# Decoder step: other paces for the background decode in the projection (7.0 to 6.4) and in the second attention (15.0 to 45)

## The chip, the cores and the metric

The kernel runs on one core of a Trainium2 chip. The metric is the device time of one launch in microseconds. The engines are TensorE (PE in the profile; PEld is its weight load), VectorE (DVE), ScalarE (ACT), GpSimd (POOL) and SyncE (SP); SP, ACT and POOL also issue DMAs.

## The reference, cut to what matters

One layer of a decoder is computed for two groups at once: a prompt of 1024 rows, and 8 sample rows that are decoded against a paged cache of 8192 past positions each.

```python
h = rmsnorm(x) @ w_in                       # q, k, v, forget logits, u, z
att = softmax(q k^T/8 + cq - ck) v          # causal, 8 heads of 64
sgu = u * (tril(w_s) z + b_s)               # gating in chunks of 128
x = x + concat(rmsnorm(att), rmsnorm(sgu)) @ w_o
x = x + cross_attend(rmsnorm(x), 256 memory tokens)
x = x + conv_ffn(rmsnorm(x))                # width 2 * 2816, conv of 3
y = rmsnorm(x)
# sample rows: the same layer, with att over the pages of the cache
k_all = concat(cache_k[page_table], k); v_all = concat(cache_v[page_table], v)
```

All values are float32. The outputs are both groups' y, the new k, v, log forget gates and the convolution's states.

## The kernel before, in words

The prompt is the main work. It goes through stages, each a Python generator: `p1` (the input projection, w_in in column groups of 512, with x split in a high and a low part, so that each product is three matmuls), `attention(0)` for rows 0 to 511 mixed with the memory's keys and the gating, `attention(1)` for rows 512 to 1023, and then for each half of the rows `merge` (the normed attention and gating rows are turned by TensorE and split, L860 and L212/L213), `out_proj` (w_o, L973 to L975), `cross` and `ffn`. The stages bear the names p1, att0, att1, mid0 (merge to cross of the first half), ffn0, mid1 and ffn1. A weight block is loaded by SP into one of four `wr` tiles (L223) and split by ScalarE (L209) and VectorE (L210) into `wh` and `wl`. The probability rows of the second attention use the same `wr` tiles.

The sample group's decode is the background. `decode()` has 148 steps. Step g loads, by an indirect DMA on POOL's queue (L1306), one K tile of 128x2048 into one of the four `kv` tiles. VectorE multiplies it by the query (L1312) and reduces it by heads (L1316); in the two attention stages each of the two operations is cut in halves (KS = 2), elsewhere it is done whole. Eighteen steps behind, the step loads one V tile into the same four `kv` tiles (L1365); every second step TensorE multiplies two V tiles (L1371, 16 matmul records). At the end of 16 steps, one sample row's pages, the softmax follows in small pieces over the next steps. After the decode, `sample_rest` does the remaining layer for the sample rows, with L1653 its last large product.

The order comes from the loop that drives both. Each yield of the main generator gives a number, about the microseconds of TensorE that were issued. The loop adds it to an account, and issues a step of the background when the account has reached the pace of the stage, which it then subtracts. Per yield it issues at most `int(t / pace) + 1` steps.

```python
acc[0] += t
most = int(t / PACE[phase[1] or phase[0]]) + 1
while bgs and not held[0] and most and acc[0] >= PACE[phase[1] or phase[0]]:
    most -= 1
    acc[0] -= PACE[phase[1] or phase[0]]
    if next(bgs[0], None) is None:
```

The yields of p1 sum to 210.0 (16 of 2.6, 8 of 5.2 in the groups Q and Z, 8 of 5.4, 16 of 5.2, 4 of 0.1), those of att0 with its fill to 124.2, those of att1 to 74.6; merge yields 0.5 eight times, and out_proj 2.6 eight times for its first column half. What is left in the account at the end of a stage is carried into the next. With the paces before, p1 issues 30 steps (0 to 29), att0 6 (30 to 35) and att1 5 (36 to 40); 3.8 units are carried on, and step 41 is issued after out_proj's first yields.

What is issued is put in order for each engine by a scheduler that goes by priority (the order of issue) among the instructions that are ready by its own model of time; the order is fixed when the kernel is built. A K step's VectorE instructions are bound behind the newest VectorE instruction that had been issued before it (`behind(ENG.DVE)`), and the value products likewise on TensorE. `close(1)`, which norms the second attention's rows, runs beside the first half's merge.

Of the kernel before, what the change touches and what calls it, by code (L numbers as in the profile page):

```python
# [72 lines left out]
KS = 2  # L73
BKQ = 1
LA = (2, 2)
PACE = {'p1': 7.0, 'att0': 20.0, 'mid0': 8.0, 'ffn0': 8.5, 'att1': 15.0, 'mid1': 6.8, 'ffn1': 2.5, 'rest': 2.9}


def build(nc, tc, ctx, a, phases=None):
# [1684 lines left out]
    for t in prompt():  # L1764
# [6 lines left out]
# [6 lines that stand above are left out]
# [94 lines left out]
```

## Time and the profile before

| what | value |
|---|---|
| median of 3 runs | 1911.37 us |
| lowest, highest | 1909.26, 1916.39 us |
| profiled execution, its own time | 1913.18 us |
| its span, first to last instruction | 1911.4 us |
| mean granted TensorE clock | 0.978 |
| HBM read, written | 493.63 MB, 21.84 MB |

In the rows of the profile a group is line, engine, operation, out<-in with shapes, count, then busy time in us and mean ns of one, then the idle time of the engine just before these instructions and what ended it. In a row by windows stand the stretch, its length, the busy time of PE, PEld, DVE, ACT and POOL with instruction counts, the granted TensorE clock, the share of time in which the 16 DMA engines were busy, and GB/s. In a row of waits stand the total in us, how often, and the longest. In a row in order of time stand start, duration, the instruction, and in brackets the idle time before it and what ended it.

### The profile page before, as it was taken

Reading aid. Unit: us, or ns where it says so; the run is one execution under the profiler, and the core shown is the slowest. Engines: PE = TensorE matmul, PEld = TensorE weight load, DVE = VectorE, ACT = ScalarE, POOL = GpSimd, SP = SyncE. Lnnn points to the kernel's source line nnn. Section 1 sums busy time; section 2 is a strip of 40 time slices with the busy share of each in tenths; the row PEclk is TensorE's granted clock in tenths of the full one; section 3 lists DMA queues with packets and bytes.
Section 4 is the critical chain, followed back from the end, with each engine's and each line's share of the span. In section 5 each row is a group of like instructions: output and inputs, shape, how many; then the busy total and the mean of one; then the engine's idle time right before and its main releaser. Section 6 shows DMA issues by size and latency. Waiting matters only on the chain.

```text
span 1911.4 us, 24216 instructions
## 1 busy us (share of the span) xinstructions
PE 1816.1 (95%) x9255; PEld 1296.3 (68%) x9255; DVE 1404.6 (73%) x1662; ACT 761.7 (40%) x1435; POOL 480.6 (25%) x429
## 2 busy tenths in 40 slices
PE   8999999778898999999999999998999999899998
PEld 5987666555676667777777776775665667667765
DVE  4888678777777887989989998887864548754344
ACT  5332356566633435333333244324353333232232
POOL 1232342222121332213432322354222012101110
PEclk9999999989998999999999999998999999899999
DMA  8777988743395876759878879888859557676872
GB/s 322 286 245 278 323 319 302 265 162 119 128 399 210 324 268 256 297 206 359 313 264 313 301 304 344 340 338 302 307 206 362 191 200 265 215 242 247 320 280 101
DMA packets 156373, 517.07 MB, mean 271 GB/s; under 512 B 20169, under 2 KB 41929, under 8 KB 123489
## 3 DMA queue, kind: packets, MB, share of 16 engines
q0 software_dynamic: 56400, 339.04, 47.7%
q1 hardware_dynamic: 92944, 163.89, 24.7%
q10 hardware_dynamic: 6912, 12.59, 1.7%
q8 instruction: 73, 1.20, 0.2%
q14 instruction: 44, 0.35, 0.1%
HBM read 493.63 MB, written 21.84 MB: 270 GB/s over the span
## 4 chain that ended last, share of the span: by engine, by line
PE 66%; DVE 8%; ACT 3%; DMA 3%; issue 2%; POOL 0%; SPq 0%; DVEq 0%; POOLq 0%; ACTq 0%
PE ba L247 9%; PE ba L246 9%; PE ba L248 9%; PE bb L246 6%; PE bb L247 5%; PE bb L248 5%; PE dv L1371 5%; DMA kv<-cache_k,kidx 2%; DVE kv L1312 1%; DVE s L1316 1%; PE dv L1614 1%; PE ba L973 1%; PE ba L975 1%; PE ba L974 1%; PE bb L772 1%
## 5 line engine op out<-in xcount | busy, mean ns | idle before, releaser
L209 ACT ACTIVATE wh<-wr 128x1024 fp32r<-128x1024 f32 (+2 forms) x220 | 228.8, 1044 | 488.8 <-PE ba L247 147.8
L210 DVE TENSOR_TENSOR wl<-wr,wh 128x1024 fp32r<-128x1024 f32 (+2 forms) x220 | 262.5, 1200 | 166.7 <-PE ba L248 71.3
L1306 POOL DMA_INDIRECT kv<-cache_k,kidx x128 | 179.8, 1405 | 545.6 <-DVE s L1316 249.3
L1312 DVE TENSOR_TENSOR kv<-kv,d 128x2048 f32<-128x2048 f32 (+1 forms) x139 | 292.3, 2113 | 28.2 <-DMA kv<-cache_k,kidx 26.9
L1316 DVE TENSOR_REDUCE s<-kv 128x32 f32<-128x2048 f32 (+1 forms) x139 | 292.0, 2106 | 0.6
L1365 POOL DMA_INDIRECT kv<-cache_v,kidx x128 | 181.3, 1416 | 424.2 <-PE dv L1371 169.6
L246 PE MATMUL ba<-wh,u 128*128 128x512 f32 (+1 forms) x596 | 226.9, 382 | 0.0
L247 PE MATMUL ba<-wl,u 128*128 128x512 f32 (+1 forms) x596 | 226.2, 380 | 0.0
L248 PE MATMUL ba<-wh,u 128*128 128x512 f32 (+1 forms) x596 | 223.4, 380 | 1.0 <-DVE u L210 1.0
L246 PE MATMUL ba<-u,wh 128*128 128x512 f32 (+2 forms) x520 | 203.0, 391 | 1.3 <-DVE u L213 1.2
L247 PE MATMUL ba<-u,wh 128*128 128x512 f32 (+2 forms) x520 | 203.8, 392 | 0.0
L248 PE MATMUL ba<-u,wl 128*128 128x512 f32 (+2 forms) x520 | 202.7, 390 | 0.0
L1371 PE MATMUL dv<-kv,s 128*32 128x512 f32 x1024 | 138.0, 618 | 6.8 <-DMA kv<-cache_v,kidx 6.8
L246 PE MATMUL bb<-u,wh 128*128 128x512 f32 (+2 forms) x344 | 138.2, 402 | 1.8 <-DVE u L213 1.8
L247 PE MATMUL bb<-u,wh 128*128 128x512 f32 (+2 forms) x344 | 136.5, 397 | 2.5 <-DVE u L213 2.5
L248 PE MATMUL bb<-u,wl 128*128 128x512 f32 (+2 forms) x344 | 135.9, 396 | 0.0
L246 PEld LDWEIGHTS ba<-wh,u 128*128 128x128 f32 x596 | 112.7, 189 | 31.4 <-issue 8.0
L248 PEld LDWEIGHTS ba<-wh,u 128*128 128x128 f32 x596 | 112.1, 189 | 29.0 <-issue 6.3
L247 PEld LDWEIGHTS ba<-wl,u 128*128 128x128 f32 x596 | 112.4, 189 | 23.8 <-issue 2.9
L247 PEld LDWEIGHTS ba<-u,wh 128*128 128x128 f32 x520 | 98.7, 190 | 33.3 <-issue 13.0
L246 PEld LDWEIGHTS ba<-u,wh 128*128 128x128 f32 x520 | 98.5, 190 | 31.7 <-issue 7.1
L248 PEld LDWEIGHTS ba<-u,wl 128*128 128x128 f32 x520 | 98.5, 189 | 28.5 <-issue 9.3
(418 smaller groups left out, 3105.5 us busy)
## 6 DMA issues: line engine op xcount, KB each, us to landing
wr<-w_up SPq DMA_DIRECT2D x88, 512.0 KB
kv<-w_up POOLq DMA_DIRECT2D x22, 1024.0 KB
wr<-w_down SPq DMA_DIRECT2D x40, 512.0 KB
kv<-w_down POOLq DMA_DIRECT2D x11, 1024.0 KB
wr<-w_in SPq DMA_DIRECT2D x16, 512.0 KB
wr<-w_o SPq DMA_DIRECT2D x16, 512.0 KB
wr<-w_cq SPq DMA_DIRECT2D x16, 512.0 KB
wr<-w_co SPq DMA_DIRECT2D x16, 512.0 KB
```

What stands on the lines that cost most here:

```text
L209: nc.scalar.activation(h, src, AF.Copy)
L210: nc.vector.tensor_tensor(l, src, h.bitcast(F32), op=ALU.subtract)
L246: mmul(out, sh, mh, start=(i == 0), stop=False)
L247: mmul(out, sh, ml, start=False, stop=False)
L248: mmul(out, sl, mh, start=False, stop=(i == n - 1))
L772: mmul(po[64 * j : 64 * j + 64, q0:256], vn[:, kt, 64 * j : 64 * j + 64], pt[j][kt // 4][:, kt % 4, q0:256], start=(kt == 0), stop=(kt == ...
L973: mmul(pss[i], mh[k][:, tb], wh, start=(k == korder[0]), stop=False)
L1306: nc.gpsimd.indirect_dma_start(kv, None, a["cache_k"], off(kidx[:, b, ch : ch + 1]))
L1312: nc.vector.tensor_tensor(kvv[:, i : i + m, :], kvv[:, i : i + m, :], qb.unsqueeze(1).broadcast_to((P, m, 512)), op=ALU.mult)
L1316: nc.vector.tensor_reduce(s[:, ch * 4 + i : ch * 4 + i + m, :].rearrange("p k h -> p (k h)"), kvv[:, i : i + m, :].rearrange("p k (h d) -> ...
L1365: nc.gpsimd.indirect_dma_start(kv, None, a["cache_v"], off(kidx[:, b, ch : ch + 1]))
L1371: mmul(dv[32 * j : 32 * j + 32, :], s[:, ch * 4 : ch * 4 + 4, :].rearrange("p k h -> p (k h)"), kvv[:, j, :], start=(ch == 0), stop=(ch == ...
```

## The change

Two entries of the pace table get other values. No instruction's work is altered apart from one thing: a K step that is issued in a stage other than the two attentions is done in whole instead of half operations.

```diff
-PACE = {'p1': 7.0, 'att0': 20.0, 'mid0': 8.0, 'ffn0': 8.5, 'att1': 15.0, 'mid1': 6.8, 'ffn1': 2.5, 'rest': 2.9}
+PACE = {'p1': 6.4, 'att0': 20.0, 'mid0': 8.0, 'ffn0': 8.5, 'att1': 45, 'mid1': 6.8, 'ffn1': 2.5, 'rest': 2.9}
```

By the loop's arithmetic p1 then issues 32 steps (204.8 of 210.0 units), att0 6 and att1 one; 39.0 units are carried into mid0, whose pace is 8.0, and each of the merge's first five yields issues a step. All later steps move with them.

## The prediction, made before the changed kernel was run

> **What bounds the kernel now.** First the page's totals and slices, for the engine that sets the end and the places where it does not run.
>
> ```profile
> PE 1816.1 (95%) x9255; PEld 1296.3 (68%) x9255; DVE 1404.6 (73%) x1662; ACT 761.7 (40%) x1435; POOL 480.6 (25%) x429
> PE   8999999778898999999999999998999999899998
> PE 66%; DVE 8%; ACT 3%; DMA 3%; issue 2%; POOL 0%; SPq 0%; DVEq 0%; POOLq 0%; ACTq 0%
> ```
>
> TensorE is busy 95% of the span and is two thirds of the chain that ended last. The change adds and removes no matrix work, so its effect is in the other 5%, and in time at a lowered clock. The dip in the slices lies at about 250 to 525 us, the two attentions. The view by windows separates the stages around the change: projection, second attention, merge and first output projection, and what follows; then three short stretches of the attention and one of the last stage.
>
> ```profile
> core 0: us, PE busy (x) PEld busy (x) DVE busy (x) ACT busy (x) POOL busy (x), PEclk, DMA share, GB/s
> 13.00:250.00 237.00, 236.92 (x1271) 184.90 (x1271) 170.24 (x152) 89.39 (x137) 67.72 (x49) 1.00 0.81 292
> 405.00:520.00 115.00, 94.00 (x625) 66.06 (x626) 82.28 (x169) 72.97 (x195) 22.52 (x31) 0.91 0.40 134
> 520.00:550.00 30.00, 29.05 (x156) 20.73 (x157) 25.20 (x29) 13.06 (x21) 8.75 (x6) 1.00 1.03 401
> 550.00:575.00 25.00, 25.00 (x117) 18.68 (x116) 17.00 (x15) 7.40 (x17) 5.26 (x4) 1.00 0.95 375
> 420.00:430.00 10.00, 7.30 (x38) 5.72 (x39) 6.29 (x16) 5.79 (x16) 0.96 (x1) 0.68 0.76 243
> 440.00:450.00 10.00, 7.21 (x49) 4.80 (x48) 8.26 (x15) 6.46 (x15) 2.25 (x3) 0.83 0.31 104
> 490.00:500.00 10.00, 6.04 (x35) 4.49 (x34) 6.66 (x16) 5.06 (x16) 1.03 (x1) 0.83 0.32 108
> 1424.00:1500.00 76.00, 76.00 (x384) 45.65 (x383) 39.64 (x59) 28.12 (x45) 16.29 (x18) 1.00 0.86 318
> ```
>
> Three things are to be seen. The projection keeps TensorE busy 236.92 of 237 us: every matmul put there is paid in full. The second attention idles it 21 of 115 us at a mean clock of 0.91, with DMA at 40%: this stage has something to win. The merge stretch (520 to 550 us) is full on all sides: TensorE 29.05, VectorE 25.20 of 30 us, DMA saturated at 401 GB/s. What leaves the attention late lands there.
>
> The waits of TensorE within 405 to 520 us name what it waits for:
>
> ```profile
> PE ba L728 <- DVE mx L736: 6.8, 1, 6.8
> PE bb L756 <- ACT wr L738: 5.0, 2, 4.0
> PE ba L728 <- ACT wr L738: 4.3, 5, 1.6
> PE ms L772 <- ACT t L763: 2.8, 1, 2.8
> ```
>
> Two waits, 6.8 and 4.0 us, are half of the 21. The time-ordered view of VectorE and TensorE shows whose they are.
>
> ```profile
> 413.75 2.34 DVE L1312 TENSOR_TENSOR kv<-kv,d 128x1024 f32<-128x1024 f32 x2
> 417.32 1.21 DVE L1316 TENSOR_REDUCE s<-kv 128x16 f32<-128x1024 f32 x1
> 419.98 1.20 DVE L1316 TENSOR_REDUCE s<-kv 128x16 f32<-128x1024 f32 x1
> 421.82 0.14 DVE L736 TENSOR_TENSOR mx<-mx 128x1 f32<-128x1 f32 x1
> 422.05 0.71 PE L728 MATMUL ba<-u,u 128*128 128x448 f32 x1 [6.78 <-DVE mx L736]
> 439.24 2.35 DVE L1312 TENSOR_TENSOR kv<-kv,d 128x1024 f32<-128x1024 f32 x2
> 460.76 2.35 DVE L1312 TENSOR_TENSOR kv<-kv,d 128x1024 f32<-128x1024 f32 x2
> 487.17 2.35 DVE L1312 TENSOR_TENSOR kv<-kv,d 128x1024 f32<-128x1024 f32 x2
> 490.83 2.33 DVE L1316 TENSOR_REDUCE s<-kv 128x16 f32<-128x1024 f32 x2
> 494.10 0.65 PE L756 MATMUL bb<-cp,wr 128*128 128x128 f32 x4 [3.96 <-ACT wr L738]
> 515.60 2.35 DVE L1312 TENSOR_TENSOR kv<-kv,d 128x1024 f32<-128x1024 f32 x2
> ```
>
> The five starts of L1312 (413.75, 439.24, 460.76, 487.17, 515.60) are the five decode steps of this attention, numbers 36 to 40. The steps at 413.75 and 487.17 sit between a score product and its row maximum, and TensorE waits behind them; the other three are beside other work.
>
> **The change part by part.** *Which steps move.* By the loop's arithmetic (the yields given above) the projection issues steps 0 to 31 instead of 0 to 29, the first attention 32 to 37 instead of 30 to 35, the second attention one step (38) instead of five. At its end 39.0 units are owed, and at pace 8.0 with one step a yield the first five yields of the merge issue steps 39 to 43 in a row. Before, 39 and 40 lie in the attention, and 41 comes after the merge. So the merge stretch gains three steps beyond its own. After it the decode stays about two steps ahead, and reaches the last feed-forward stage at step 131 instead of 129. Step 38 is issued at 370.2 units, near the 376.6 of before (the step at 460.76), so the four that leave are those at 413.75, 439.24, 487.17 and 515.60.
>
> *The attention.* The step at 413.75 spends 2.34 + 1.21 + 1.20 = 4.75 us on VectorE ahead of the L736 that ended the 6.78 us wait; without it some 2.0 us of that wait are left, because L733, L795 and L713 lie there too. The step at 487.17 spends 2.35 + 2.33 = 4.68 us in the same place, more than the wait of 3.96: all of it goes, and ScalarE's exponentials (L738, waits of up to 1.6 us) are next. The steps at 439.24 and 515.60 bring nothing: the first wait behind 439 is ScalarE's L763, and nothing long follows 515. Gain 4.75 + 3.96 = 8.7 us. From below: nothing, if ScalarE is late in both places anyway; from above: these 8.7 and the 2.8.
>
> *The clock.* The windows that hold these waits granted 0.68 and 0.83: 3.2 and 1.7 us of full-speed time lost in 10 us each, 4.9 together. I take half, 2.5, because 440 to 450 us also shows 0.83 though its longest wait is 2.8 us, so a wait cut to 2 us can still cost clock. Ends: 0 and 4.9. The Trainium skill ("TensorE: Matmul & The Clock Gate", What's actually happening) puts the lowered clock behind an idle window of about 3.4 us. By that rule both losses vanish and the sum gains 2.4 us more; the 0.83 behind a wait of 2.8 us speaks against using it as a threshold here.
>
> *The steps' own price elsewhere.* Full-size operations and their neighbours:
>
> ```profile
> L1312 DVE TENSOR_TENSOR kv<-kv,d 128x2048 f32<-128x2048 f32 x117 | 266.5, 2282 | 28.2 <-DMA kv<-cache_k,kidx 26.9 <-PE bb L1106 0.8 <-issue 0.2
> L1316 DVE TENSOR_REDUCE s<-kv 128x32 f32<-128x2048 f32 x117 | 265.7, 2275 | 0.6
> L210 DVE TENSOR_TENSOR wl<-wr,wh 128x1024 fp32r<-128x1024 f32 x208 | 252.0, 1219 | 158.8 <-PE ba L248 70.4 <-PE bb L248 35.0 <-PE ba L247 19.3
> 515.09 1.92 PE L1371 MATMUL dv<-kv,s 128*32 128x512 f32 x16
> 1855.96 1.03 PE L1653 MATMUL ms<-kv,d 128*32 128x512 f32 x4
> ```
>
> A step is 2.28 + 2.28 = 4.56 us of VectorE; every second step a pair of value steps runs on TensorE for 1.92 us; and each step loads one K and, 18 steps behind, one V tile of 1.05 MB on POOL's queue.
>
> *The projection.* Two more steps: 9.1 us of VectorE against 237 - 170 = 67 idle, and about 4 MB, 10 us at 401 GB/s, against a DMA share of 0.81: hidden by TensorE's 237 us. One more value pair on a full TensorE costs 1.9. If the weight splits of L210 were caught behind the steps, the 9.1 would be the upper end; below zero nothing leads, since no wait there can shrink.
>
> *The merge.* Three more steps are 13.7 us of VectorE where 520 to 550 us leaves 4.8 idle: 8.9 over, with the splits of w_o (L210, 1.2 us each) and of the turned rows (L213) in the same queue, and the output projection waiting for both. The two first steps find their tiles loaded, because four KV buffers fill in the attention, whose DMA share is 0.40. The products of the first row blocks cover some of the delay; 25 us later 8 us of VectorE are idle again, but TensorE's lost time is not got back. Ends: 0, all hidden, and 8.9 plus a clock loss of 1.7. I take 7, nearer to the upper end, because 29.05 of 30 us leave no idle time in which to catch up. The value pair of 515.09 moves from the end of the attention to here: TensorE pays it in both places, no net cost.
>
> *The end.* The last stage starts full too (76 of 76 us) and has one value pair less, -1.9, against the +1.9 of the projection. The decode's remainder ends with L1653 at 1857 us, 54 us before the span does, so that an earlier finish brings nothing.
>
> Sum: -8.7 - 2.5 + 1.9 + 7 - 1.9 = -4.2 us. The profiled execution took 1913.2 us (span 1911.4, 1.8 around it); it becomes 1909.0. The median of the runs is 1911.4, 1.8 below the profiled one: 1907.
>
> **The rivals.** *The burst is hidden.* The scheduler may slip steps 39 and 40 into the attention's tail, where VectorE is idle 33 of 115 us, away from row maxima. Then the merge costs nothing and the clock term is whole: -8.7 - 4.9 = -13.6, 1898. For it: order on an engine is by readiness, and the tiles are there. Against: a step is bound behind the newest VectorE instruction issued before it, which for step 39 is already one of the merge.
>
> *The burst stops TensorE.* VectorE runs its queue in order. If the steps that still wait for their tiles stand ahead of the splits of w_o, TensorE has only the row blocks already split. Price: the three steps whole, 13.7, the landing of two tiles, 2.1 MB at 401 GB/s, 5.2, and a clock loss like that of 420 to 430 us, 3.2: 22.1 in place of 7, so +10.9, 1922. It decides from the point at which a step's L1312 with a tile on its way stands ahead of the second w_o split. For it: L1312's 26.9 us of waits for K tiles. Against: these stand over 117 operations, a quarter microsecond each.
>
> *The loads get in each other's way.* Three steps bring 6.3 MB more into a stretch at 401 GB/s; if all of it delays w_o and x, that is 15.7 us in place of the 7: +4.5, 1916. The Trainium skill ("DMA: Bandwidth & Descriptors", Issuing engines are not separate DMA queues) says that transfers share the same 16 engines and interleave whichever engine issued them, which speaks against this change; the saturated 1.03 agrees. Against the full price: four tiles come early, in the attention's idle DMA time.
>
> *Nothing moves.* The steps wait for buffers and data, and so run where they ran: 1911.
>
> **How the numbers follow.** A measurement of this kernel tells about 0.5% from no change, 9.6 us: faster is below 1901.8, slower above 1920.9. Chances: forecast 0.49 (its own range, from the ends of its terms, 1898 to 1914), hidden burst 0.20, stopped TensorE 0.19, loads 0.08, nothing moves 0.04. The range 1895 to 1924 holds the forecast, both rivals' values and leaves out their far ends: a merge dearer still, or a gain beyond 13.6 with other waits of the attention gone. Faster: most of the hidden burst and a corner of the forecast, 0.24. Slower: most of the stopped TensorE and the far end of the loads, 0.22. Same: 0.54.
>
> **What would show it.** In the changed profile the attention should hold one or two L1312 pairs, not five, with the 6.8 and 4.0 us waits at most 2 us and a clock above 0.91; TensorE still 100% busy in the projection; and four or five full-size L1312 close together in the merge, with TensorE waiting a few microseconds on L213 or L210. No such waits means the hidden burst; more than 10 us there, with L1312 waiting for K tiles, the stopped TensorE. The forecast is wrong in its first term if the attention gets no shorter, in its fourth if the merge's loss is not between 0 and 11 us, and in its approach if the difference arises after 610 us.

## The result, and the profile after

The changed kernel takes 1916.54 us (median of 20 runs, 1906.19 to 1925.28), the kernel before 1911.33 us beside it (20 runs, 1906.80 to 1916.39). The ratio is 1.0024, with a 95% interval of 1.0012 to 1.0035: slower by 5 us, within the 0.5% that the prediction counted as no change, and on the other side of zero than its forecast of 1907. The profiled execution took 1917.93 us (span 1916.2, mean clock 0.977) against 1913.18 (1911.4, 0.978).

The page of the kernel after: totals, TensorE's slices and the chain that ended last.

```profile
PE 1817.0 (95%) x9255; PEld 1294.5 (68%) x9255; DVE 1400.5 (73%) x1654; ACT 763.5 (40%) x1435; POOL 496.2 (26%) x429
PE   8999997879989989999999999999999999899998
PE 77%; DMA 8%; DVE 7%; issue 5%; ACT 2%; POOL 0%; SPq 0%; DVEq 0%; POOLq 0%; ACTq 0%
```

The totals say nothing: TensorE is busy for 1816.1 us before and 1817.0 after. TensorE's slices of 47.9 us do: the seventh (287 to 335 us) has gone from 9 to 7, the tenth and eleventh (431 to 527) from 8 to 9, the twelfth (527 to 575) from 9 to 8. Windows of the kernel after, in the order of the prediction's, with the border between projection and first attention added (PE, PEld, DVE, ACT, POOL busy, clock, DMA share, GB/s):

```profile
13.00:250.00 237.00, 235.00 (x1270) 179.36 (x1269) 176.23 (x152) 84.12 (x126) 78.21 (x50) 1.00 0.83 303
290.00:303.00 13.00, 3.57 (x16) 2.12 (x17) 9.54 (x12) 2.27 (x3) 6.50 (x6) 0.53 1.03 403
405.00:520.00 115.00, 103.24 (x697) 73.06 (x696) 77.44 (x187) 86.59 (x237) 19.56 (x29) 0.95 0.32 103
420.00:430.00 10.00, 7.56 (x44) 5.40 (x44) 6.93 (x17) 8.28 (x23) 2.26 (x3) 0.86 0.15 57
520.00:550.00 30.00, 22.92 (x120) 14.71 (x121) 23.64 (x26) 11.62 (x21) 6.72 (x6) 0.83 0.98 371
```

The same 13 us at the border, before:

```profile
290.00:303.00 13.00, 13.00 (x71) 9.69 (x70) 12.68 (x14) 7.97 (x16) 6.02 (x7) 1.00 1.01 399
```

Three things are to be seen. The attention did what was forecast: TensorE busy 103.24 instead of 94.00 of 115 us, clock 0.95 instead of 0.91. The merge lost 6.1 us of TensorE and 0.17 of the clock. And at 290 to 303 us, where the prediction had put no wait at all, TensorE runs 3.57 of 13 us at a clock of 0.53.

To add the stages up, each kernel's main work (all TensorE columns outside the decode) was summed in order of time, and the time compared at which it reaches the amount that before has reached at a given moment. Kernel after: 16.9 us late at 310 us, 1.9 early at 520, 10.2 late at 530, 4.8 late at the end. So projection with its border costs 16.9, the attentions give 18.8 back, the start of the merge takes 12.1, and what follows returns 5.4. At 280 us the main work is 0.5 us late, so the 16.9 arise within 30 us.

The waits of TensorE in the kernel after, first at the border (280 to 310 us), then in the second attention (405 to 520), then in the merge (520 to 550); us in total, times, longest:

```profile
PE ba L677 <- DMA t<-q_d: 5.7, 1, 5.7
PE ms L1335 <- DVE pm L1329: 5.3, 1, 5.3
PE ms L756 <- DVE m L1338: 0.9, 1, 0.9
...
PE ba L728 <- ACT wr L738: 4.6, 3, 2.8
PE bb L756 <- ACT wr L738: 2.4, 2, 1.7
...
PE dv L1371 <- DMA kv<-cache_v,kidx: 5.6, 1, 5.6
PE ba L973 <- DVE u L213: 1.3, 1, 1.3
```

In the attention the waits of 6.8 and 4.0 us are gone and ScalarE's L738 is what is late next. In the merge it is a V tile. At the border the rows in order of time, VectorE then TensorE, show the two waits:

```profile
285.85 2.28 DVE L1312 TENSOR_TENSOR kv<-kv,d 128x2048 f32<-128x2048 f32 x1
288.16 2.29 DVE L1316 TENSOR_REDUCE s<-kv 128x32 f32<-128x2048 f32 x1
290.48 0.69 DVE L1327 TENSOR_TENSOR s<-s,dec 128x512 f32<-128x512 f32 x1
291.21 1.07 DVE L1329 TENSOR_REDUCE pm<-s 128x8 f32<-128x512 f32 x1
292.33 0.37 PE L1335 MATMUL ms<-cp,pm 128*8 128x128 f32 x1 [5.33 <-DVE pm L1329]
302.04 1.11 PE L677 MATMUL ba<-cp,t 128*128 128x128 f32 x4 [5.67 <-DMA t<-q_d]
```

Step 31 is the last of a sample row's 16. With the new pace it is issued inside the projection. The transposing matmul of that row's softmax (L1335) is issued with step 32, at the start of the first attention, and stands in TensorE's queue at the border; step 31's own 4.57 us of VectorE and two operations more (L1327, L1329) must end first. Behind it TensorE comes to L677, which turns q of the next pair of heads, and that load is late too. Its issue and first use, in before and after:

```profile
283.94 0.37 SPq L664 DMA_DIRECT2D t<-q_d  x1
291.17 0.66 PE L677 MATMUL ba<-cp,t 128*128 128x128 f32 x4
```

```profile
286.06 0.37 SPq L664 DMA_DIRECT2D t<-q_d  x1
```

Before, it is issued at 283.94 and had landed 1.7 us ahead of its use, after 5.6 us; after the change it is issued 2.1 us later and takes 15.9 us. What else the DMA engines had to move is seen in POOL's issues of decode tiles, first before, then after:

```profile
270.70 1.52 POOL L1365 DMA_INDIRECT kv<-cache_v,kidx  x1 [0.30 <-issue]
284.18 1.01 POOL L1306 DMA_INDIRECT kv<-cache_k,kidx  x1 [6.17 <-DVE s L1316]
```

```profile
278.48 1.73 POOL L1306 DMA_INDIRECT kv<-cache_k,kidx  x1 [0.71 <-DVE s L1316]
284.96 0.95 POOL L1365 DMA_INDIRECT kv<-cache_v,kidx  x1 [4.75 <-PE bb L756]
```

Before, no tile is asked for in the 13 us ahead of the q load, and POOL's queue moves 0.56 MB between q's issue and its landing. After, tiles are asked for 7.6 and 1.1 us ahead of it, and the queue moves 3.51 MB in that time. The first of q's packets starts 1.9 us after the issue in the one case and 8.1 us in the other.

### The profile page after: what moved, and what is told of

Read it like the earlier page. It is cut to its first block, busy times and chain, and to the rows that moved or that the text cites. A ratio compares the mean times of both kernels' runs of the same rounds, so it can differ in the third digit from the quotient of the medians.

```text
span 1916.2 us, 24261 instructions
## 1 busy us (share of the span) xinstructions
PE 1817.0 (95%) x9255; PEld 1294.5 (68%) x9255; DVE 1400.5 (73%) x1654; ACT 763.5 (40%) x1435; POOL 496.2 (26%) x429
## 4 chain that ended last, share of the span: by engine, by line
PE 77%; DMA 8%; DVE 7%; issue 5%; ACT 2%; POOL 0%; SPq 0%; DVEq 0%; POOLq 0%; ACTq 0%
PE ba L246 12%; PE ba L247 12%; PE ba L248 12%; PE bb L246 6%; PE bb L247 6%; PE bb L248 6%; PE dv L1371 5%; DMA kv<-cache_v,kidx 2%; DVE kv L1312 1%; PE ba L973 1%; PE dv L1614 1%; DMA zg_d<-t 1%; PE ba L975 1%; DVE s L1316 1%; PE ba L974 1%
## 5 line engine op out<-in xcount | busy, mean ns | idle before, releaser
L1306 POOL DMA_INDIRECT kv<-cache_k,kidx x128 | 198.6, 1552 | 522.5 <-PE dv L1371 199.5
L1316 DVE TENSOR_REDUCE s<-kv 128x32 f32<-128x2048 f32 (+1 forms) x135 | 291.7, 2164 | 0.4
L1371 PE MATMUL dv<-kv,s 128*32 128x512 f32 x1024 | 135.8, 606 | 9.5 <-DMA kv<-cache_v,kidx 9.3
L248 PEld LDWEIGHTS ba<-wh,u 128*128 128x128 f32 x596 | 112.8, 189 | 27.5 <-issue 3.8
L247 PEld LDWEIGHTS ba<-u,wh 128*128 128x128 f32 x520 | 98.2, 189 | 34.1 <-issue 10.9
```

The lines of the kernel that those rows point to most:

```text
L247: mmul(out, sh, ml, start=False, stop=False)
L248: mmul(out, sl, mh, start=False, stop=(i == n - 1))
L1306: nc.gpsimd.indirect_dma_start(kv, None, a["cache_k"], off(kidx[:, b, ch : ch + 1]))
L1316: nc.vector.tensor_reduce(s[:, ch * 4 + i : ch * 4 + i + m, :].rearrange("p k h -> p (k h)"), kvv[:, i : i + m, :].rearrange("p k (h d) -> ...
L1371: mmul(dv[32 * j : 32 * j + 32, :], s[:, ch * 4 : ch * 4 + 4, :].rearrange("p k h -> p (k h)"), kvv[:, j, :], start=(ch == 0), stop=(ch == ...
```

## The experiments

The first question was which of the two numbers makes the loss, the second what the steps owed at the end of the attention do, the third why two steps more in the projection cost so much. Each run has a label (e1, f4), which stands beside its time or its pace; where nothing else is said a ratio is to the kernel before, measured beside it, with its 95% interval.

**One number at a time.**

```diff
-'p1': 7.0 ... 'att1': 15.0
+'p1': 6.4 ... 'att1': 15.0
```

> The projection's pace alone (6.4), the second attention stays at 15.0. Theory: the two extra steps bring the end of sample row 1 (steps 31 to 33, its softmax) to the border between projection and first attention, where TensorE waits for VectorE (5.3 us) and for q (5.7 us); in the changed kernel main work was 17 us late at 310 us. So this part alone is slower than before by 4 to 15 us, with TensorE waits of 8 us or more at 280 to 300 us, and it has no loss at the merge. Rival (the loss is made by the attention's pace and its debt alone): within 2 us of before.

Measured (e1) 1920.95 us, ratio 1.0052 (1.0034 to 1.0070), a loss of 10 us as the theory had it. The border's waits are there, 5.3 us for the softmax and 2.0 for q; the main work is 18.9 us late at 310 us and still 14.0 late at 520.

```diff
-'p1': 7.0 ... 'att1': 15.0
+'p1': 7.0 ... 'att1': 45
```

> The second attention's pace alone (45), the projection stays at 7.0: one step in the attention, then four in the merge's first four yields, 41 in all at its end, as before. Theory: the attention gets 8 to 12 us shorter, the merge 8 to 11 us longer with a wait of TensorE for a V tile (L1371); 1908 to 1914 in all, and no TensorE waits over 3 us at 280 to 300 us. Rival (the projection's steps are harmless, the debt makes the whole loss): slower than before by 4 us or more.

Measured (e2) 1891.02 us, ratio 0.9894 (0.9873 to 0.9914), far below both the theory and the rival. The attention's pace alone gains 20 us, the projection's alone costs 10, and together they cost 5: the change is a good half and a bad half, and the bad one costs 25 us beside the good one. Windows of e2, border and then attention:

```profile
270.00:310.00 40.00, 36.94 (x183) 26.62 (x182) 32.59 (x38) 24.54 (x50) 10.88 (x11) 0.92 1.00 382
405.00:520.00 115.00, 100.35 (x692) 70.52 (x693) 83.89 (x169) 81.26 (x206) 21.67 (x29) 0.97 0.44 150
520.00:550.00 30.00, 30.00 (x137) 22.61 (x136) 23.34 (x22) 7.96 (x15) 8.72 (x6) 1.00 1.01 404
```

Its main work is 21.5 us early at 520 us and 17.0 early at 530, with four steps in a row in the merge. The merge's price is 4.5 there, against 12.1 in the kernel after.

**The debt.** Here the account is cut at the end of the second attention, so that no burst follows; the steps cut off come later, at the paces of the later stages.

```diff
             phase[0] = f"mid{hf}"
+            if hf == 0:
+                acc[0] = min(acc[0], 3.8)
```

With 7.0 and 45:

> As the attention's pace alone, but the debt of the account is cut to 3.8 units at the merge, so that no burst is issued there and the decode runs four steps later from then on. Theory: the attention's gain stays and the merge's loss goes: 1899 to 1905. Rival (the merge's loss comes of anything but the burst, or the attention's gain is only late work caught up): within 3 us of the attention's pace alone, or of before.

Measured (e3) 1918.88 us, ratio 1.0051 (1.0032 to 1.0069). With 6.4 and 45:

> Both paces of the change, with the debt cut to 3.8 units at the merge. Theory: the changed kernel less the merge's loss, so 6 to 11 us below its 1916.5: 1905 to 1911, with the waits at 280 to 300 us still there. Rival (the burst is not what costs): 1914 to 1919.

Measured (e4) 1925.66 us, ratio 1.0083 (1.0059 to 1.0106). Both expectations are missed: without the burst the kernel is slower by 28 us in the one case and by 9 in the other. In e3 the merge still costs 6.7 us (21.8 early at 520, 15.1 at 530); what is lost lies at the end. The decode is four steps behind, and its remainder is now what ends last: e3's last rows of L1653, with those of before for comparison.

```profile
1899.17 1.06 PE L1653 MATMUL dv<-kv,d 128*32 128x512 f32 x4 [0.59 <-DMA kv<-w_down]
1900.05 1.03 PE L1653 MATMUL ms<-kv,d 128*32 128x512 f32 x4
```

```profile
1879.67 1.06 PE L1653 MATMUL dv<-kv,d 128*32 128x512 f32 x4
1880.56 1.03 PE L1653 MATMUL ms<-kv,d 128*32 128x512 f32 x4
```

Before, these products run between matmuls of the main work; in e3 TensorE's main work ends at 1865.3 us, and from then on it waits for one w_down tile after the other. The prompt's last norm, on ScalarE and VectorE, stands behind the remainder's instructions there and runs from 1905 to 1916 us. So the burst with 7.0 is not a cost to be avoided but what keeps the decode from becoming the end. In e4 the remainder ends 25 us ahead of the span's end; its main work is 0.7 us early at 1000 us and 6.4 late at 1400, and what takes that was not followed.

```diff
-                acc[0] = min(acc[0], 3.8)
+                acc[0] = min(acc[0], 16.0)
```

(6.4 and 45, two steps in a row instead of five.)

> The changed kernel with the debt cut to 16 units at the merge: two steps in a row there instead of five, 41 steps at its end as in the kernel before, so that no pair of value products is reached before its V tiles have landed. Theory: the V tile wait of 5.6 us and its half clock go, the wait for the turned rows stays; main work is 3 to 7 us earlier at 540 us than in the changed kernel, 1909 to 1914 in all if the decode's remainder does not become the end. Rival (the place of the burst does not matter): 1915 to 1918.

Measured (g4) 1912.42 us, ratio 1.0001 (0.9982 to 1.0020), 4 us better than the whole change. The wait for the V tile in the merge is gone (waits of TensorE, 515 to 560 us):

```profile
PE ba L973 <- DVE u L213: 2.2, 2, 1.4
PE bb L772 <- DVE u L761: 0.8, 1, 0.8
```

Longer bursts, with 7.0 in the projection:

```diff
-'p1': 7.0 ... 'att1': 15.0
+'p1': 7.0 ... 'att1': 100
```

> Projection at 7.0, the attention at 100: no step in the second attention, and a debt of 78.8 units, so that the merge issues eight steps in its eight yields instead of four. If a burst at the merge costs by itself, its loss doubles: TensorE waits over 8 us at the merge, 1898 to 1912. If the burst is hidden and what the merge loses is the turning of the rows behind a shorter attention, as the run without debt says: 1887 to 1895, the merge's waits as with four steps.

Measured (f4) 1887.23 us, ratio 0.9870 (0.9832 to 0.9908), the fastest median. Eight steps in a row in and after the merge, and TensorE's longest wait there is 2.4 us, for L213:

```profile
PE ba L973 <- DVE u L213: 2.4, 1, 2.4
PE ba L246 <- ACT wh L209: 1.0, 1, 1.0
```

So the length of a burst is not what costs in the merge; a value pair whose V tile has not landed when its turn comes does. This holds for the merge alone: between 640 and 830 us, in the cross attention, f4's main work falls back by 20 us (21.7 early, then 2.2), and gains them back by 1600.

```diff
-'p1': 7.0 ... 'att1': 15.0
+'p1': 7.0 ... 'att1': 25
```

> Projection at 7.0, the attention at 25: three steps in the second attention instead of five or one, no debt. Theory: the attention's gain goes by the steps taken out, 17 to 21 us for four, so 8 to 11 us for two: 1900 to 1905, if the decode's remainder does not become the end (it runs two steps later than before). Rival (single steps at a bad place make the gain): within 3 us of 1911 or of 1891.

Measured (f5) 1908.41 us, ratio 0.9973 (0.9959 to 0.9987), as the rival had it. The profiled execution took 1899.1 us, the fastest of the run. In it, with three steps left in the attention, the main work is 21.1 us early at 520, as with one. The three lie at 417.6, 454.3 and 494.6 us, none of them ahead of a row maximum that TensorE waits for (longest waits, 405 to 520 us):

```profile
PE ba L728 <- ACT wr L738: 3.7, 3, 1.6
PE bb L772 <- ACT t L763: 2.8, 1, 2.8
```

So in this trace the gain of the attention does not go by the number of steps; where two of them fall at pace 15 accounts for it. Where the other executions lose the 9 us by which the median is longer is not recorded.

**The border.** The softmax of a row is moved one step later (`soft_all`, `soft_exp`, `soft_sum` at chunks 1, 2, 3 instead of 0, 1, 2), with 6.4 and 45 (the first of the three lines):

```diff
-            if ch == 0 and 1 <= b < 9:
+            if ch == 1 and 1 <= b < 9:
                 dg[b - 1] = soft_all(b - 1, pm[b - 1])
```

> The changed kernel (6.4 and 45) with the softmax pieces of each sample row (its maximum, its exponentials, its sum) issued one step later than now, so that TensorE's part of row 1's softmax no longer stands at the border between projection and first attention. Theory: the wait of 5.3 us for VectorE's row maxima (L1329) and a part of the 17 us at half clock behind it go: 1902 to 1910, against 1916.5 of the changed kernel. Rival (the two extra steps cost by their load on VectorE and DMA, wherever the softmax stands): 1914 to 1919.

Measured (f1) 1922.93 us, ratio 1.0055 (1.0034 to 1.0076). The wait for the softmax is gone, and the load of q takes its place, larger (waits of TensorE, 275 to 325 us):

```profile
PE ba L677 <- DMA t<-q_d: 13.1, 1, 13.1
PE ms L772 <- ACT u L763: 0.7, 1, 0.7
```

The load of q is asked for two score tiles earlier, with 6.4 and 45:

```diff
-LD = [(0, 1, 0), (0, 0, 0)]
+LD = [(0, 0, 0), (0, 0, 0)]
```

> The changed kernel (6.4 and 45) with the first attention's loads of the next pair of heads (q, k, v) issued two score tiles earlier. In the run with the later softmax the wait for row maxima was gone, and the wait for this q load (16 us from issue to landing, 5.6 before) took its place and was 13 us long. Theory of the q load: the load lands before TensorE needs it, its wait (5.7 us) goes, the softmax wait of 5.3 us stays: 1906 to 1913 against 1916.5. Rival (the load is late at whatever point it is issued, because it shares the DMA engines with the tiles of the steps): 1914 to 1920.

Measured (g1) 1913.73 us, ratio 1.0008 (0.9989 to 1.0028). The load is issued at 282.2 instead of 286.1 and takes 14.7 us instead of 15.9: asked for earlier, it stays slow, behind a tile that POOL had asked for 2.5 us before it. Both edits together:

> Both at once: the changed kernel with the earlier q load and the softmax pieces one step later. Theory: both waits at 285 to 303 us and the half clock behind them are gone: 1898 to 1906. Rival (a third thing is late at the same place): above 1912.

Measured (g2) 1919.17 us, ratio 1.0054 (1.0035 to 1.0073); 8.9 us late at 310 instead of 16.9, but still 6.3 us of waiting for q, and at 520 and 530 (1.2 early, 11.4 late) as the whole change. So taking away one wait, or shortening both, does not bring the time back: main work that is 8 us earlier at 310 us is no earlier at 520. The earlier load beside the fastest version (7.0 and 100):

> Projection at 7.0, the attention at 100 (1887 without more) with the q load earlier, as the fastest version that the runs so far point to. There TensorE does not wait for this load, so within 3 us of 1887.

Measured (g3) 1887.84 us, ratio 0.9871 (0.9851 to 0.9890): no difference where the load was in time.

**The projection's pace.** All of these with 45 in the attention; the first has one step more than 7.0.

```diff
-'p1': 7.0
+'p1': 6.7
```

> The attention's pace 45 with the projection at 6.7, half way: 31 steps in the projection, so that step 31, the last of sample row 1, comes in the first attention. Theory of the border: close to the attention's pace alone (1891), 1889 to 1897, no wait for row maxima at 285 to 295 us. Rival (load, in proportion to the steps added): half way between 1891 and 1916, 1901 to 1907.

Measured (f2) 1894.95 us, ratio 0.9902 (0.9867 to 0.9937). Then 6.2 (h1), 6.1 (h3) and 7.4 (f8) in its place:

> Projection's pace 6.2 (33 steps there), second attention's 45. With 7.0 and 45 (30 steps) 1891.0 was measured, with 6.7 (31 steps) 1894.9, with 6.4 (32 steps) 1916.5. If each step that the projection takes on has a price of its own, 33 steps cost more than 32: 1920 to 1930. If the price hangs on where the softmax of a row and the load of q fall against the border between projection and first attention, the time need not rise: row 1's logits end inside the projection at 198.4 of its 210 units, the exponentials still fall at the border: 1903 to 1916.

> Projection's pace 6.1 (34 steps), second attention's 45. Price per step: 1930 to 1940, as four steps more than 7.0 gives. Place of the softmax: row 1's softmax is issued at 201.3 and 207.4 of 210 units, so that its wait of 5.3 us at the border is gone and the load of q is the only one left: 1900 to 1910.

> Projection's pace 7.4 (28 steps), second attention's 45. Price per step: two steps fewer than 7.0 save as much as two more cost, 1870 to 1880. Place at the border: nothing of row 1 is near it, as with 7.0, so 1888 to 1895. If the decode's remainder, now some 22 us ahead of the last output product, becomes the end because the decode is two steps later: 1897 to 1910.

Measured 1901.34 us, 0.9941 (0.9923 to 0.9959); 1905.91 us, 0.9956 (0.9936 to 0.9977); 1931.91 us, 1.0104 (1.0072 to 1.0136). A price per step falls: two steps fewer than 7.0 are the dearest of all, three and four more are cheaper than two. That the row's softmax at the border decides falls too, since 7.4 has none there and loses 10.3 us by 310. The longest waits of TensorE at the border (270 to 330 us), 6.1 and then 7.4:

```profile
PE bb L756 <- ACT t L738: 10.0, 2, 9.8
```

```profile
PE ba L677 <- DMA t<-q_d: 11.5, 1, 11.5
```

With 6.1 the exponentials (L738) stood in ScalarE's queue behind a store (L551, issued at 287.05 us) and a norm's sum of squares (L204). The store's issue had waited for the load of v, asked for at 267.8 us, to land at 286.98; one row of ScalarE:

```profile
287.42 0.63 ACT L204 ACTIVATE junk<-t 128x512 bf16<-128x512 f32 x1 [10.30 <-DMA u<-o_v]
```

Two paces with as many steps as 6.4 and 6.1, but the last step at the end of the projection, as 7.0 has it (k1 and k2):

```diff
-'p1': 7.0
+'p1': 6.56
```

> Projection's pace 6.56, second attention's 45: 32 steps in the projection as with 6.4, but the last is issued at 209.9 of its 210 units (6.4: 204.8), where with 7.0 the last of 30 lies too, and the next comes 20 units later in the first attention. If the price hangs on where the steps fall against the border, it goes and the time is near that of 7.0 and 45: 1888 to 1898. If it hangs on the number of steps, on row 1's softmax coming early, or on the bytes: 1910 to 1920 as with 6.4.

```diff
-'p1': 7.0
+'p1': 6.17
```

> Projection's pace 6.17, second attention's 45: 34 steps, the last at 209.8 of 210 units. With 6.1 (34 steps, the last at 207.4) 1905.9 was measured. Place against the border decides: 1888 to 1898. Number of steps or the row they belong to decides: 1902 to 1910 as with 6.1.

Measured 1914.30 us, 1.0032 (1.0016 to 1.0048), and 1896.56 us, 0.9923 (0.9898 to 0.9948). The place of the last step helps in the second case by 9 us against 6.1, in the first by 2: there row 1's softmax comes at the border once more, with a wait of 5.6 us for L1329. So the place alone does not decide either.

Last, 6.4 with 100 in the attention:

> Projection's pace 6.4 (32 steps), second attention's 100 (no step there). If the price of the projection's pace and the gain of the attention's add up, as they did with 45: 1887.2 plus 25.5, 1913. If the longer debt, all repaid in the merge, makes the row of V tiles come early enough that its wait of 5.6 us goes: 1904 to 1908.

Measured (h2) 1920.92 us, ratio 1.0041 (1.0025 to 1.0057), 34 us above 7.0 with 100, so neither expectation holds. Without a step in the attention the merge is cheap (3.7 early at 520, 2.8 at 530). The price comes back in the cross attention: the main work goes from 5.5 early at 640 us to 26.9 late at 830. The longest waits of TensorE there explain only a part of it:

```profile
PE dv L1371 <- DMA kv<-cache_v,kidx: 6.1, 1, 6.1
PE ms L1359 <- DVE lp L1353: 2.6, 1, 2.6
```

The profiled executions side by side; us late (+) or early (-) in the main work against before, and the difference of the spans:

| p1, att1 | steps in p1 | 310 | 360 | 520 | 530 | 1400 | span | longest wait at the border |
|---|---|---|---|---|---|---|---|---|
| 7.0, 45 | 30 | 0.7 | -1.4 | -21.5 | -17.0 | -24.3 | -22.5 | none above 2.5 |
| 7.0, 100 | 30 | 1.2 | 2.7 | -17.7 | -16.6 | -14.5 | -27.4 | L738, 5.1 |
| 7.4, 45 | 28 | 10.3 | 17.5 | -5.2 | 5.4 | 11.0 | 15.5 | q, 11.5 |
| 6.7, 45 | 31 | 10.0 | 16.9 | -6.0 | -5.1 | -12.2 | -18.0 | q, 4.9 |
| 6.56, 45 | 32 | 11.2 | 14.5 | 2.8 | 7.2 | -0.8 | -4.1 | softmax, 5.6 |
| 6.4, 45 | 32 | 16.9 | 24.7 | -1.9 | 10.2 | 10.9 | 4.8 | q, 5.7 and softmax, 5.3 |
| 6.2, 45 | 33 | 17.5 | 23.4 | 5.7 | 6.2 | -2.4 | -8.0 | L763, 3.0; softmax, 2.8 |
| 6.17, 45 | 34 | 17.3 | 15.0 | -6.4 | -1.9 | -8.5 | -15.9 | L738, 6.3 |
| 6.1, 45 | 34 | 25.5 | 27.5 | -3.9 | 0.5 | 6.4 | -6.7 | L738, 9.8 |

Shown: every pace of the projection that was tried beside 7.0 is 10 to 26 us late at 310 us, with fewer steps as with more, and it is not always the same thing that TensorE waits for longest. Between 360 and 520 all of them win 12 to 31 us back; 7.0 with 45 wins 20 there.

Why q lands after some 5 to 7 us with 7.0 and after 10 to 16 with every other pace can be read from the traces. In the six with 7.0 (before, e2, e3, f4, f5, g3) POOL had asked for its last tile 8 us or more ahead of the q load, and its queue moved 0.1 to 0.7 MB between q's issue and its last packet. In the other fourteen a tile had been asked for at most 5.5 us ahead, and the queue moved 1.4 to 3.8 MB. POOL asks for a K tile when an earlier step's reduction (L1316) frees the tile: at 284.18 us before, at 278.48 after. So what matters is where these moments fall beside the load, and that shifts with the pace in either direction. This is read from traces: no run held the tiles back at an unchanged pace.

Not settled: a rule from which the loss of a given pace could be told beforehand, and why what comes after 530 us differs by some 20 us between paces (6.7 gains 13 there by span, 7.4 loses 10). The lateness at 310 us does not decide the time either: 6.17 is as late there as 6.4 and ends 20 us earlier.

## Why the prediction was wrong

By its own steps, terms of the sum against the main work's lateness of the kernel after; the value pairs' own time (L1371) is taken out of each.

| step | predicted | measured |
|---|---|---|
| projection and border | +1.9, one value pair | +16.9, of which 1.5 value pairs |
| attention and its clock | -8.7 - 2.5 = -11.2 | -18.8, of which -3.9 value pairs: -14.9 |
| merge | +7 | +12.1, of which 3.9 value pairs: +8.2 |
| what follows | -1.9 | -5.4, of which -3.8 value pairs |
| sum | -4.2 | +4.8 |

**The projection is the step that failed.** Its term was +1.9, its upper end 9.1, and 16.9 were measured. Its working holds where it was made: in 13 to 250 us TensorE is busy 235.00 instead of 236.92 of 237 us, and at 280 us the main work is 0.5 us late, so the two steps' VectorE time and loads are hidden there. But it ended the argument with that window. The steps do not end with the projection: those issued in its last units run at the border, where the first attention's small matmuls already stand in the queue, the DMA is saturated (1.03), and TensorE's order is fixed. The sentence "below zero nothing leads, since no wait there can shrink" was true and no bound from above; the rows of 250 to 310 us were not part of the argument. No rival held this either. The one named "the loads get in each other's way" had the mechanism, late transfers at a saturated DMA, and put it in the merge; that its 1916 is the measured time is luck. Luck is also that the sum missed by no more than 9 us: 15 us too little at the border stand against a gain of the attentions that was forecast 7.6 too small, value pairs included. The two are not independent, as g2 shows, so the split holds for this kernel and not for each part alone.

**The attention** was right in place and cause and too small: the waits of 6.8 and 4.0 us went, the clock rose to 0.95 (e2: 0.97), and L738 with 2.8 and 1.7 us is next, as was said. The term was -11.2 against -14.9 in the kernel after and some -18.3 in e2 (from 0.7 late at 310 to 21.5 early at 520, less 3.9 of value pairs). f5 bears out the reading that two of the steps made the waits: with three steps left, none in those places, its trace is as early at 520.

**The merge** came out at its size, 8.2 against 7 and within 0 to 11, but not by its reason. VectorE's 8.9 us above its idle time were not what TensorE waited for: 1.3 us for L213, and 5.57 for a V tile that the burst had just asked for.

```profile
526.16 1.80 POOL L1365 DMA_INDIRECT kv<-cache_v,kidx  x1 [38.84 <-PE dv L1371]
537.62 1.94 PE L1371 MATMUL dv<-kv,s 128*32 128x512 f32 x8 [5.57 <-DMA kv<-cache_v,kidx]
```

The tile was issued at 526.16, its product stood ahead of main work in TensorE's queue, and 530 to 543 us ran at a clock of 0.62. With eight steps in the merge (f4), with two (g4) and with five at the projection's pace 6.7 (f2), no such wait is there. The rival "the burst stops TensorE" had this shape, an instruction in an in-order queue whose tile is on its way, on the wrong engine; its time of 1922 is not what the burst costs, since 7.0 with a burst is the fast version. The hidden burst (1898) came nearest for 7.0: e2 took 1891.02.

**The end.** The prediction put the last L1653 at 1857 us, 54 us ahead of the end; the row it showed was not the last. That is at 1880.56, 30 us ahead. In e3, where the decode comes four steps later, this cover is used up, and the span still lasts 19 us beyond the last L1653; so some 11 of the 30 us were spare. For this change it made no error, as the decode comes earlier; for the reverse it would have.

**The clock.** The prediction weighed the rule of the Trainium skill ("TensorE: Matmul & The Clock Gate", What's actually happening) that an idle window of some 3.4 us lowers the clock, and took half. The kernel after agrees with that rule where waits are long: 5.33, 0.95 and 5.67 us at the border are followed by a granted 0.53. The attention's 420 to 430 us, whose longest wait is 2.36 us, still shows 0.86, so that 3.4 us is no safe side here. Of the loads, the rule of the Trainium skill that all queues share 16 engines ("DMA: Bandwidth & Descriptors", Issuing engines are not separate DMA queues) agrees with q's 15.9 us at a DMA share of 1.03, beside 3.51 MB of tiles. The prediction used it for the merge and not for the border.

## What to carry to other kernels

When background work is issued by a pace, read the border behind the stage that receives it, not only the stage: what is issued last there runs in the next one, in front of its small dependent instructions. A stage that is full and hides everything is no cover for its neighbour. A pace that leaves a border without waits may be a coincidence, so test both directions of it before putting a price on the work moved, and split a change of two numbers into its parts: here 7.0 with 100 takes 1887.23 us, 0.987 of before, and the gain of the changed kernel's better half was hidden by the other.

## What the runs showed of the hardware

The same load of q on SP's queue took 5.6 us from issue to landing before and 15.9 us after the change. The DMA share was full in both cases (1.05 and 1.03 in these stretches), but 0.56 MB of tiles on POOL's queue moved beside it in the one and 3.51 MB in the other; issuing it 3.9 us earlier gave 14.7.

The clock fell to 0.53 over 290 to 308 us behind waits of 5.33, 0.95 and 5.67 us. It stayed there in the last 5 of these us, in which TensorE was busy all the time, and was 1.00 again in the next 5:

```profile
303.00:308.00 5.00, 5.00 (x17) 3.98 (x17) 1.94 (x3) 4.74 (x10) 0.00 (x0) 0.53 0.72 263
```

So the cluster of waits cost its own length and, in the full stretch behind it, some 2.4 us of full-speed time more (5 us at 0.53).
